# Two more classes may fall within a pair, one class is gone, and some code is aligned and ordered anew: a nested self-attention kernel on one core

## The chip, the cores and the metric

The kernel runs on one core of a Trainium2 chip. The metric is the time of one execution on the device in microseconds (us); before the change the median of three runs is 331.35 us (331.15 to 332.71). PE is the matrix engine (TensorE), DVE is VectorE, ACT is ScalarE, POOL is GpSimd; SP (SyncE) here issues most of the loads, the transposes and part of the stores.

## The reference

The reference is self-attention over 32 sequences of different lengths, eight heads of 64:

```python
for b in range(batch):
    seq_len = lengths[b]
    x_b = x[b, :seq_len].copy()
    qkv = np.matmul(x_b, w_qkv)
    q, k, v = np.split(qkv, 3, axis=-1)
    # each to (n_heads, seq_len, head_dim)
    scores = scale * np.matmul(q, k.transpose(0, 2, 1))
    scores_max = np.max(scores, axis=-1, keepdims=True)
    attn = np.exp(scores - scores_max)
    attn = attn / (np.sum(attn, axis=-1, keepdims=True) + 1e-08)
    out_b = np.matmul(attn, v).transpose(1, 0, 2).reshape(seq_len, dim)
    output[b, :seq_len] = out_b
```

The output is zero from `seq_len` on. x is 32 x 512 x 512 in float32. The lengths are drawn at random from 64 to 511, with a fixed seed; sorted from long to short they are 502 447, 446 436, 363 357, 351 347, 343 333, 323 315, 310 261, 260 257, 246 230, 223 220, 216 183, 164 152, 143 140, 134 119, 101 86, 79 75.

## The kernel before

**Sorting and classes.** The prologue sorts the sequences on the device, longest first, and takes them in 16 pairs, as they stand above. A pair has a class, the smallest number of rows in `CLASSES` (96 to 512 in steps of 32, and 340) that holds its first sequence. Both sequences of a pair are worked at that number of rows. Where the second one fits the next lower class, the pair may "fall": its second half is worked at the lower class. `drops` lists the classes that may fall; before, these are classes of at most 384 rows whose next lower class has as many tiles of 128 rows. A code per pair, twice the class's place in the list plus one where the pair falls, is worked out on the device: POOL makes the column `inner` (1 for thresholds to which a pair may fall, -99 for others), PE multiplies it with the comparisons `le`, and DVE makes `codes` from it.

**Bodies.** For every class there is code for one pair, written by `make_body(N, M, W)`: N rows in the first half, M in the second, W for the batch that is projected in the second half. A half, `half(pr, h, T, N, W, st)`, attends one sequence (scores on PE into `psc`, exponentials on ACT into `ep`, products with `v_aug` on PE into `pav` or `pa`, division on DVE into `onat`) and, in the same stretch of code, projects the next sequence (Q, K and V from `xT` and `w_r`, moved out of PSUM by DVE and ACT). The order of these pieces is written out by hand as a string of tokens for each number of tiles T (`ORDER`, `DENSE`, `FOUR`, `FOUR_SIDES`): at T = 4 with 512 or 480 rows it is `ORDER[4]`, with 448 or fewer one of the `FOUR` strings, in which projections run in two row halves side by side ("cross" products). Where the last tile holds at most 64 rows (`half_rows`), its V projection is made in two column halves side by side (`vsides`). With one tile (T = 1) a half is 32 projections, eight attention products, one V projection and the scores of the next sequence.

**What follows what.** `graph` lays the classes out one behind another, for PE, ACT and DVE each; register compares on the pair's code lead from one body to the next. For PE, targets of jumps are marked ahead (`hint`, `expect`) and code is aligned (`align`); for ACT and DVE one alignment stands at the lead of the first class (`LEAD`). Two-tile pairs keep their scores in another layout than one-tile pairs, so between them PE runs `bridge`: it makes the scores of the next sequence anew in the one-tile layout. `settled` stands beside it.

**Feeding.** SP works by the class alone and doesn't see falls: for each sequence it loads x (`load`), waits until POOL has cast it to f16 (`s_xc`) and until PE is done with the old `xT` (`s_xtf`), and issues a transposing DMA for each tile (`to_xT`), all in its own order, with stores between them. A sequence is loaded five ahead and transposed about two ahead. At one tile, SP transposes into a spare part of `xT` (`stage`) and POOL copies it into place.

**Prologue.** While weights and the first two sequences arrive, DVE casts and copies; behind the last V of the first sequence it makes the two mask tables (`mask_table`, for all 32 sequences) and reads its first code (`begin_loops`).

Of the kernel before, what the change touches and what calls it, by code (L numbers as in the profile page):

```python
# [13 lines left out]
P = 128  # L14
NH = 8
HD = 64
NPAIR = 4
# [14 lines left out]
CLASSES = sorted([STEP * k for k in range(3, 17)] + [DENSE_ROWS], reverse=True)  # L32
FETCH = 256
LEAD = {"act": 0, "dve": 52}


class Prog:
# [52 lines left out]
    def run_part(self, e, a, b, then=None, late=None):  # L90

        b = len(self.ops["pe"]) if b is None else b
        wide = self.wide(a, b)
        for k in range(a, b):
            self.ops["pe"][k](e)
            if then is not None and k == wide[0]:
                then()
            if late is not None and k == wide[-1]:
                late()
# [62 lines left out]
def kernel(  # L162
# [518 lines left out]
    def attn_one(pr, h, ends):  # L681
# [21 lines left out]
        for j in range(2):  # L703
            pr.take("dve", s_od[h][j], 16)

# [17 lines left out]
        for done, w in enumerate(parts):  # L723
            mult(w, done)

# [34 lines left out]

    def half(pr, h, T, N, W, st, last=False):

        g = 1 - h
        tiles = -(-W // P)
        pr.signals += [s_vf[g]] if T == 1 else [s_xtf[h], s_vf[g]]
# [16 lines left out]
        if T == 1:  # L782
            start_proj()
            qk(pr, "a0", g, [(i, 0) for i in range(NPAIR)], W, P)
            qk(pr, "a1", g, [(i, 1) for i in range(NPAIR)], W, P, "act")
            attn_one(pr, h, False)
            vwhole(pr, g)
            read_class(pr, h)
            for b in ("a0", "a1"):
                acquire(pr, b)  # L790
            pr.signals.append(s_xtf[g])
            pr.take("pe", s_on[g])
            scores(pr, h, g, 0, 0, 1, W)
            act_store(pr, h, 0, T)
            return
# [21 lines left out]
        for tok in toks:  # L817
# [40 lines left out]
            elif k == "O":  # L858
                if T == 2 and h == 1:
                    pr.take("act", s_of[0][1])  # L860
                    pr.add("act", lambda e: store(
                        e, e.snap(regs_act["first"], min_val=0, max_val=B - 1), 0, 1, T))
# [3 lines left out]
            else:  # L866
# [36 lines left out]
                for b in bs:  # L903
                    give(b)
                    st["holds"][b] = (g, i) if k in "FGHIQKqk" else (g, "V")
# [37 lines left out]
    def make_body(N, M, W, last=False, turn=None):  # L943
# [50 lines left out]
    def make_prologue():  # L994
# [98 lines left out]
        copy(1, "dve")  # L1093
        cast_x(2)
# [64 lines left out]
        for tok in "Q2 K2 S0 S1 Q3 K3 V0 S2 S3 V1 X2 V2 X3 V3".split():  # L1159
# [25 lines left out]
        pr.add("dve", mask_table)  # L1185
        pr.take("pe", s_on[0])
        return pr

# [23 lines left out]
    def mask_table(e):  # L1212
        q = Chain(e, s_self)
        mask(q, masks[:, 0:B, 0, :], n_k[:, 1 : B + 1])
        mask(q, masks[:, 0:B, 1, :], n_s[:, 0:B])
        q.signal(s_tab)
# [5 lines left out]
    def turn(N):  # L1222
        order = list(stay[lower[N]].middle)
        if is_dense(N) != is_dense(lower[N]):
# [4 lines left out]
    drops = {N: make_body(N, lower[N], lower[N], turn=turn(N)) for N in CLASSES  # L1229
             if lower[N] < N and -(-lower[N] // P) == -(-N // P) and N <= 3 * P}  # L1230
    drops_to = [lower[N] for N in drops]
# [47 lines left out]
    def graph(e, name, opening=None, before=None):  # L1279
# [13 lines left out]
        def align(N, slots, off=0):  # L1293
# [5 lines left out]
            elif 3 * P < N <= FOUR_ROWS:  # L1299
                slot = AT_FOUR  # L1300
# [5 lines left out]
        drop = [N in drops for N in CLASSES]  # L1306
        assert tiles[n - 3 :] == [2, 1, 1]
# [7 lines left out]
        marks = {}  # L1315
# [20 lines left out]
        def goes(k, part, c):  # L1336

            if c == 2 * k + 2:
                return part == "drop"
            if c == 2 * k + 3:  # L1340
                return k + 1 < n and drop[k + 1]
            return k + 2 < n and (k + 2 != one or before is None)
# [52 lines left out]
        def lay_drop(k):  # L1395

            N, body = CLASSES[k], drops[CLASSES[k]]
            codes = (2 * k + 3, 2 * k + 4, 2 * k + 2)
# [3 lines left out]
            if tiles[k] == 1:  # L1402
                if fetch:
                    body.run_part(e, 0, body.second[name], lambda: entry(k))
                else:
                    body.run_half(name, e, 0)
                leave_ = label(k, "gone") if fetch else label(n, "bye")
                e.br_cmp(cur, 2 * n, label(k, "dropped"), leave_, "IS_NE")
                if fetch:
                    bye(k, "gone")  # L1410
                open_(label(k, "dropped"))
                body.run_half(name, e, 1)
                e.br(label(k + 1, "first"))
                return
            if fetch:
                body.run_part(e, 0, body.second[name], lambda: entry(k),
                              lambda: expect("drop", k, codes))
            else:
                body.run_half(name, e, 0)
            body.run_half(name, e, 1)  # L1420
            if goes(k, "drop", codes[0]):
                go("drop", k, codes[0], label(k + 1, "drop"), label(k, "drop_b"))
                open_(label(k, "drop_b"))
            go_first("drop", k, k + 1, label(k, "drop_c"))
            open_(label(k, "drop_c"))
            if goes(k, "drop", codes[1]):
                go_first("drop", k, k + 2, label(k, "drop_d"))
                open_(label(k, "drop_d"))
            align(N, SECOND, -1)
            e.br(label(k + 1, "tail"))  # L1430

        def tail(k):
# [4 lines left out]
            if before is not None and k + 2 == one:  # L1437
                e.br_cmp(cur, 2 * one, label(k + 1, "tail"), label(k + 1, "lead"), "IS_GE")
# [20 lines left out]
        for k, N in enumerate(CLASSES):  # L1459
            T, codes = tiles[k], (2 * k + 3, 2 * k + 4)  # L1460
            final_class = k == n - 1
            if not final_class:
# [3 lines left out]
                if not fetch and k == 0:  # L1466
# [680 lines left out]
```

## Time and profile before

| | |
|---|---|
| runs | 332.71, 331.35, 331.15 us; median 331.35 |
| profiled execution, span on the core | 330.1 us, 1.25 below the median of the runs |
| PE busy | 316.4 us (96%) |
| ACT busy | 242.4 us (73%) |
| DVE busy | 203.6 us (62%) |
| POOL busy | 68.7 us (21%) |
| DMA | 72.42 MB, mean 219 GB/s |
| first pair (0), on PE | 24.56 to 62.84 us |
| pair 13 on PE, its two halves | 300.13 to 310.67 us; the bridge up to 311.96 |

The span runs from the first to the last instruction of the profiled execution. A row of the timeline gives the start in us, the busy time, the engine, the source line, the operation, output<-input, and the count; in brackets the idle time ahead of it and what ended it. DVEq, ACTq, SPq and so on are the engines' sequencers, which wait for semaphores and issue DMAs.

### The profile page before, as it was taken

Reading aid. Unit: us, or ns where it says so; the run is one execution under the profiler, and the core shown is the slowest. Engines: PE = TensorE matmul, PEld = TensorE weight load, DVE = VectorE, ACT = ScalarE, POOL = GpSimd, SP = SyncE. Lnnn points to the kernel's source line nnn. Section 1 sums busy time; section 2 is a strip of 40 time slices with the busy share of each in tenths; the row PEclk is TensorE's granted clock in tenths of the full one; section 3 lists DMA queues with packets and bytes.
Section 4 is the critical chain, followed back from the end, with each engine's and each line's share of the span. In section 5 each row is a group of like instructions: output and inputs, shape, how many; then the busy total and the mean of one; then the engine's idle time right before and its main releaser. Section 6 shows DMA issues by size and latency. Waiting matters only on the chain. (4 is left out here: it accounts for less than half of the span.)

```text
span 330.1 us, 12320 instructions
## 1 busy us (share of the span) xinstructions
PE 316.4 (96%) x4353; PEld 205.5 (62%) x4354; DVE 203.6 (62%) x587; ACT 242.4 (73%) x358; POOL 68.7 (21%) x135
## 2 busy tenths in 40 slices
PE   7899999999999999999999999999999999999880
PEld 2565445455565656656666677677777777677750
DVE  3576576656585575576476557655755566767662
ACT  4577878788889879878778887787677676566531
POOL 3452220201111201210220222022111131131331
PEclk9999999999999999999999999999999999999996
DMA  6957599987656996985997999897689979965952
GB/s 195 341 138 263 94 375 310 292 179 279 153 194 142 326 263 145 323 286 149 283 314 169 235 319 216 214 291 235 212 139 174 214 199 183 170 201 148 200 145 70
DMA packets 83289, 72.42 MB, mean 219 GB/s; under 512 B 41660, under 2 KB 64188, under 8 KB 83204
## 3 DMA queue, kind: packets, MB, share of 16 engines
q1 hardware_dynamic: 69700, 58.27, 70.0%
q10 hardware_dynamic: 13504, 13.11, 11.8%
q8 instruction: 42, 0.69, 0.8%
q14 instruction: 43, 0.35, 0.4%
HBM read 25.32 MB, written 36.70 MB: 188 GB/s over the span
## 5 line engine op out<-in xcount | busy, mean ns | idle before, releaser
L367 ACT ACTIVATE ep<-psc 128x896 f16<-128x896 f32 (+9 forms) x184 | 146.8, 847 | 44.0 <-PE psc L324 34.0
L324 PE MATMUL pa<-xT,w_r 128*128 128x160 f16 (+19 forms) x952 | 127.8, 277 | 1.2 <-PEq L62 1.2
L324 PEld LDWEIGHTS pa<-xT,w_r 128*128 128x128 f16 (+1 forms) x952 | 73.0, 97 | 29.2 <-issue 10.1
L324 PE MATMUL psc<-qkT 64*128 64x224 f16 (+17 forms) x700 | 66.7, 285 | 0.6 <-ACT ep L408 0.4
L324 PE MATMUL pa<-w_r,xT 128*128 128x512 f16 (+4 forms) x332 | 58.6, 328 | 0.3 <-DVE v_aug L560 0.3
L324 PE MATMUL pav<-xT,w_r 64*128 64x352 f16 (+12 forms) x384 | 58.3, 306 | 0.0
L440 DVE CAST qkT<-pa 128x512 f16<-128x512 f32 (+9 forms) x59 | 33.4, 566 | 40.0 <-PE pa L324 36.2
L408 ACT ACTIVATE ep<-psc 128x864 f16<-128x864 f32 (+3 forms) x56 | 49.7, 946 | 10.9 <-PE psc L324 6.5
L324 PE MATMUL pav<-v_aug,ep 128*128 128x65 f16 x1268 | 54.9, 194 | 1.7 <-PEq L62 1.7
L1968 POOL MEMSET v_aug<- 128x256 f16 x28 | 8.8, 313 | 225.5 <-POOLq L1519 225.5
L324 PEld LDWEIGHTS pav<-v_aug,ep 128*128 128x128 f16 x1268 | 48.8, 98 | 10.0 <-issue 3.0
L439 ACT CAST qkT<-pa 128x320 f16<-128x320 f32 (+8 forms) x74 | 34.2, 466 | 16.6 <-PE pa L324 10.8
L661 DVE SCALAR_TENSOR_TENSOR onat<-pav,masks,rcp 128x128 f32<-128x128 f32 (+1 forms) x120 | 41.4, 384 | 4.1 <-DVE rcp L638 1.6
L1962 POOL CAST x<-x_nat 128x1536 f16<-128x1536 f32 (+3 forms) x33 | 42.0, 1272 | 8.6 <-POOLq L1519 8.3
L324 PEld LDWEIGHTS psc<-qkT 64*128 64x128 f16 x700 | 26.7, 94 | 27.2 <-issue 16.7
L463 DVE TENSOR_TENSOR v_aug<-pa,masks 128x512 f16<-128x512 f32 (+1 forms) x46 | 30.8, 674 | 15.0 <-PE pa L324 14.4
L324 PEld LDWEIGHTS pav<-xT,w_r 64*128 64x128 f16 (+1 forms) x384 | 29.8, 95 | 11.6 <-issue 1.6
L324 PEld LDWEIGHTS pa<-w_r,xT 128*128 128x128 f16 (+2 forms) x332 | 22.9, 99 | 18.3 <-issue 4.9
L324 PE MATMUL pav<-w_r,xT 128*128 128x512 f16 (+3 forms) x132 | 24.0, 333 | 0.0
L638 DVE RECIPROCAL rcp<-pav 128x8 f32<-128x8 f32 (+2 forms) x66 | 12.9, 195 | 17.5 <-PE pav L324 14.7
L324 PEld LDWEIGHTS pa<-v_aug,ep 128*128 128x128 f16 x524 | 19.3, 98 | 6.3 <-issue 2.6
L440 DVE CAST qkT<-pav 128x352 f16<-128x352 f32 (+7 forms) x27 | 14.4, 539 | 14.1 <-PE pav L324 13.4
(99 smaller groups left out, 181.4 us busy)
## 6 DMA issues: line engine op xcount, KB each, us to landing
out_dram<-zt SPq DMA_DIRECT2D x16, 768.0 KB, 5.7
x_nat<-in_x_dram SPq DMA_DIRECT2D x12, 512.0 KB
out_dram<-onat ACTq DMA_DIRECT2D x21, 256.0 KB, 3.8
x_nat<-in_x_dram SPq DMA_DIRECT2D x5, 1024.0 KB
out_dram<-onat ACTq DMA_DIRECT2D x12, 384.0 KB, 4.8
out_dram<-onat SPq DMA_DIRECT2D x12, 384.0 KB, 4.4
x_nat<-in_x_dram SPq DMA_DIRECT2D x17, 256.0 KB, 6.5
x_nat<-in_x_dram SPq DMA_DIRECT2D x4, 768.0 KB
```

The lines of the kernel that those rows point to most:

```text
L324: return lambda e: e.matmul(o, lhsT, rhs, start=start, stop=stop)
L367: return e.activation(out=dst[at], in_=src[at], func=AF.Exp, scale=scale)
L408: lambda e, par=par, b=b: e.activation(out=ep[:, i, par, 0:T, 0:N], in_=psc_f[:, par, 0 : T * N].rearrange("p (t n) -> p t n", n=N), func= ...
L439: return lambda e: e.copy(out=dst, in_=src)
L440: return lambda e: e.tensor_copy(out=dst, in_=src)
L463: return lambda e: e.tensor_tensor(out=v_aug[h][:, t, lo // HD : lo // HD + n, 0:HD], in0=area[b][:, 0:w].rearrange("p (a d) -> p a d", d=HD),
L638: pr.add("dve", lambda e: e.reciprocal(out=rv, in_=den).then_inc(s_r, 1))
L661: ins = e.scalar_tensor_tensor(scalar=now[0][:, 1, t : t + 1], op0=ALU.mult, op1=ALU.mult, **ops)
L1962: e.tensor_copy(out=x16[h][:, 0:T, :], in_=x_nat[h][:, 0:T, :]).then_inc(s_xc[h], 1)
L1968: e.memset(v_aug[h][:, T - 1, NPAIR:NH, 0:HD], 0.0)
```

## The change

- The class of 480 rows is gone; the one below 512 is 448.
- A pair of class 512 may fall to 448, and one of 160 to 128, from two tiles to one. For these `drops_at` names where each class falls to.
- A pair that falls from two tiles to one gets new code: behind its first half `fall` makes the scores of the second sequence in the one-tile layout, and `half_one` (what `half` did at T = 1, now a function) runs the second half. DVE clears the second tile of `onat` there, since SP and ACT still store two tiles. After such a pair there is no `bridge`.
- PE marks the jump into the fall of 512 ahead, in the prologue (`hint_drop`). In the falls with four tiles the marks of the next jumps are set in the second half, after some 100 matmuls.
- ACT's and DVE's code is aligned at the lead of the second class (448) instead of the first, at other offsets.
- DVE makes the mask tables behind the copy of tile 1, without the semaphore waits of `Chain` between them, and reads its first code behind K2.

The core of the diff:

```diff
-CLASSES = sorted([STEP * k for k in range(3, 17)] + [DENSE_ROWS], reverse=True)
+CLASSES = sorted([STEP * k for k in range(3, 17) if k != 15] + [DENSE_ROWS], reverse=True)
-LEAD = {"act": 0, "dve": 52}
+LEAD = {"act1": 62, "dve1": 90}
...
+        if falls:
+            pr.add("dve", lambda e: e.memset(onat[h][:, :, 1, :], 0.0))
...
+        if falls:
+            pr.add("dve", lambda e: e.memset(small, 0.0).then_inc(s_of[h][1], 1))
...
+    def half_one(pr, h, W, falls=False):
+
+        g = 1 - h
+        pr.signals.append(s_vf[g])
+        pr.take("pe", s_xt[g], 64)
+        pr.signals.append(s_x16f[g])
+        qk(pr, "a0", g, [(i, 0) for i in range(NPAIR)], W, P)
+        qk(pr, "a1", g, [(i, 1) for i in range(NPAIR)], W, P, "act")
+        attn_one(pr, h, False, falls)
+        vwhole(pr, g)
+        read_class(pr, h)
+        for b in ("a0", "a1"):
+            acquire(pr, b)
+        pr.signals.append(s_xtf[g])
+        pr.take("pe", s_on[g])
+        scores(pr, h, g, 0, 0, 1, W)
+        if falls:
+            store_first(pr)
+        act_store(pr, h, 0, 2 if falls else 1)
+
+    def fall(pr, st, M):
+
+        for b, (_, what) in st["holds"].items():
+            if what != "V":
+                acquire(pr, b)
+        acquire(pr, "s0")
+        pr.signals.append(s_xtf[1])
+        scores(pr, 0, 1, 0, 0, 1, M)
...
-            half(pr, h, T, (N, M)[h], (M, W)[h], st, last and h == 1)
+            if h and T == 2 and M <= P:
+                half_one(pr, h, W, True)
+            else:
+                half(pr, h, T, (N, M)[h], (M, W)[h], st, last and h == 1)
+            if not h and T == 2 and M <= P:
+                fall(pr, st, M)
...
         pr.add("dve", first_masks)
         copy(1, "dve")
+        pr.add("dve", mask_table)
...
+            if tok == "K2":
+                pr.add("dve", lambda e: begin_loops(e))
             if tok == "Q2":
                 pr.add("pe", lambda e: begin_loops(e))
+                pr.add("pe", hint_drop)
...
-        pr.add("dve", mask_table)
...
+    drops_at = {N: M for N, M in lower.items()
+                if M < N <= 3 * P and (-(-M // P) == -(-N // P) or M == P)}
+    drops_at.update({N: FOUR_ROWS for N in CLASSES if N > FOUR_ROWS})
...
-    drops = {N: make_body(N, lower[N], lower[N], turn=turn(N)) for N in CLASSES
-             if lower[N] < N and -(-lower[N] // P) == -(-N // P) and N <= 3 * P}
+    drops = {N: make_body(N, M, M, turn=turn(N, M)) for N, M in drops_at.items()}
...
-            elif 3 * P < N <= FOUR_ROWS:
+            elif N > 3 * P:
                 slot = AT_FOUR
...
-                if not fetch and k == 0:
-                    e.addr_align(FETCH // 2, offset=LEAD[name], max_nops=0)
+                if f"{name}{k}" in LEAD:
+                    e.addr_align(FETCH // 2, offset=LEAD[f"{name}{k}"], max_nops=0)
```

**First place, PE, the second half of pair 0.** The names: `psc` scores, `pa` and `pav` the banks that hold projections and attention products, `xT_0` the next sequence. Before, the second half that leads out of class 512:

```order
L324 MATMUL psc<-qkT_1 128x512 x4
L324 MATMUL pa<-xT_0,w_r 128x480
L324 MATMUL pav<-v_aug_1,ep 128x65 x8
L324 MATMUL pa<-xT_0,w_r 128x480
L324 MATMUL pav<-v_aug_1,ep 128x65 x8
L324 MATMUL pa<-xT_0,w_r 128x480
L324 MATMUL pav<-v_aug_1,ep 128x65 x8
```

After, the end of the first half and the begin of the second in the body that falls from 512 to 448:

```order
L327 MATMUL psc<-qkT_1 128x448 x4
L327 MATMUL pa<-w_r,xT_1 64x256 x8
L327 MATMUL pa<-xT_1,w_r 128x448 x4
L327 MATMUL psc<-qkT_1 128x448 x2
L327 MATMUL pav<-xT_0,w_r 128x448
L327 MATMUL pa<-xT_0,w_r 128x448
L327 MATMUL pav<-xT_0,w_r 128x448
L327 MATMUL pa<-xT_0,w_r 128x448
```

The last V tile of the first half is now `64x256 x8` (`vsides`), and the second half starts with cross products of 448 columns in both banks, where attention products stood between projections.

**Second place, PE, the second sequence of pair 13 and what follows.** Before, the second half that leads out of class 160 (the bridge's eight scores stand behind it, after jumps):

```order
L324 MATMUL psc<-qkT_1 128x160 x8
L324 MATMUL pa<-xT_0,w_r 128x128 x16
L324 MATMUL pav<-v_aug_1,ep 128x65 x16
L324 MATMUL pa<-xT_0,w_r 128x128 x8
L1241 ISA
L1245 TENSOR_LOAD codes
L324 MATMUL psc<-qkT_1 128x160 x4
L324 MATMUL psc<-qkT_0 128x128 x4
L324 MATMUL pa<-w_r,xT_0 128x256 x4
L324 MATMUL pa<-xT_0,w_r 128x128 x8
L324 MATMUL pav<-v_aug_1,ep 128x65 x16
L324 MATMUL pa<-w_r,xT_0 128x256 x4
```

After, the second half of the body that falls from 160 to 128:

```order
L327 MATMUL psc<-qkT_1 128x128 x8
L327 MATMUL pa<-xT_0,w_r 128x128 x32
L327 MATMUL pav<-v_aug_1,ep 128x65 x8
L327 MATMUL psc<-w_r,xT_0 128x512 x4
L1286 ISA
L1290 TENSOR_LOAD codes
L327 MATMUL psc<-qkT_0 128x128 x8
L1393 COMPARE_AND_BRANCH x3
```

The first row is `fall`. Attention takes 8 products instead of 32, and there are 16 scores instead of 16 and the bridge's 8; the eight that `bridge` made stand in the last row of matmuls.

**Third place, DVE, the prologue.** Before, the work behind the first sequence's V:

```order
L532 TENSOR_TENSOR v_aug<-pa,masks 128x4x2x64
L151 TENSOR_TENSOR masks<-row_f,n_k 128x32x4
L151 TENSOR_TENSOR masks<-row_f,n_s 128x32x4
L1257 TENSOR_LOAD codes
L1457 UNCONDITIONAL_BRANCH
```

After, from the first copy on:

```order
L1066 COPY xT<-psc 128x4x128
L1234 TENSOR_TENSOR masks<-row_f,n_k 128x32x4
L1234 TENSOR_TENSOR masks<-row_f,n_s 128x32x4
L1105 CAST x_0<-x_nat 128x512
L1105 CAST x_0<-x_nat 128x256
L1066 COPY xT<-psc 128x2x128
L1093 CAST qkT<-pa 128x512 x2
L1093 CAST qkT<-pav 128x512 x2
L443 CAST qkT<-pa 128x512 x2
L1302 TENSOR_LOAD codes
L443 CAST qkT<-pa 128x512
```

The tables stand ahead of the casts of tiles 2 and 3, and the read of the codes between the evacuations of K2 and Q3.

More of the change, by code (lines that the diff above doesn't have):

```diff
@@ L679, in attnv, with attn_one @@
         return todo
-    def attn_one(pr, h, ends):
+    def attn_one(pr, h, ends, falls=False):
         for v in (f"s{h}",) + halves_av:
@@ L782, in half @@
         if T == 1:
[L783 to L794, printed above, removed]
+            half_one(pr, h, W)
             return
@@ L1212, in mask_table @@
     def mask_table(e):
[L1213 to L1216, printed above, removed]
+        mask(e, masks[:, 0:B, 0, :], n_k[:, 1 : B + 1])
+        mask(e, masks[:, 0:B, 1, :], n_s[:, 0:B])
+        e.nop().then_inc(s_tab, 1)
     stay = {N: make_body(N, N, N) for N in CLASSES}
@@ L1314, in graph @@
         mids = {k: [] for k in range(n)}
-        marks = {}
+        marks = {("tail", -1, 1): [regs["opened"]]} if fetch else {}
         def hint_mid(k):
@@ L2109, in _ @@
             prologue.run("dve", e)
-            begin_loops(e)
             graph(e, "dve")
```

99 lines of the change are left out of this document (64 added, 35 removed).

## The prediction

> **What bounds the kernel now.** I read the page first, then PE's waits, then the stretches of the pairs that the change touches, then the rows around them.
>
> ```profile
> span 330.1 us, 12320 instructions
> PE 316.4 (96%) x4353; PEld 205.5 (62%) x4354; DVE 203.6 (62%) x587; ACT 242.4 (73%) x358; POOL 68.7 (21%) x135
> PE pav L324 <- PEq L62: 1.7, 2, 1.0
> PE pa L324 <- PEq L62: 1.2, 2, 0.9
> PE psc L324 <- ACT ep L408: 0.4, 1, 0.4
> ```
>
> PE is busy 96% of the span. Its waits inside the loops are three lines: 0.4 us behind ACT, and 1.7 and 1.2 us in its own sequencer at L62, the wait that `take` puts in. So up to the last pairs, time taken from PE is time taken from the end, unless what feeds PE then comes late. The span is 330.1 us and the median of the runs 331.35: the sum is made on the span, and the 1.25 us around it are kept.
>
> Columns of the next view: stretch, its length, busy time of PE (instructions), PEld, DVE, ACT, POOL, clock, DMA.
>
> ```profile
> 24.56:43.95 19.39, 19.39 (x210) 9.47 (x210) 12.42 (x28) 15.50 (x16) 4.31 (x4) 1.00 0.71 197
> 43.95:62.84 18.89, 18.89 (x209) 9.61 (x208) 12.48 (x34) 15.24 (x16) 2.29 (x3) 1.00 1.14 314
> 62.84:80.43 17.59, 17.57 (x245) 10.05 (x245) 10.89 (x33) 14.33 (x20) 2.29 (x3) 1.00 0.88 263
> 300.13:305.95 5.82, 5.82 (x93) 4.37 (x92) 4.20 (x13) 3.66 (x7) 1.44 (x3) 1.00 0.66 205
> 305.95:310.67 4.72, 4.72 (x89) 3.97 (x88) 3.04 (x9) 3.47 (x7) 1.43 (x3) 1.00 1.15 158
> 310.67:311.96 1.29, 0.41 (x10) 0.26 (x10) 1.15 (x3) 0.16 (x1) 0.00 (x0) 1.00 0.81 196
> 311.96:314.81 2.85, 2.85 (x53) 2.11 (x53) 1.49 (x4) 1.41 (x3) 1.38 (x3) 1.00 0.54 166
> ```
>
> In order: pair 0 (two halves at 512 rows; the next batch is projected at 512 columns, then 480), the first half of pair 1 (all at 448), pair 13 (two halves at 160, projecting 160, then 128 columns), the bridge, and the first half of pair 14. PE fills every stretch but the bridge, at a clock of 1.00.
>
> **Pair 0.** The lengths are 502 and 447, so the pair may now fall to 448. Its first half still attends 502 rows, but projects batch 1 at 448 columns. 512 to 480 columns took the half from 19.39 to 18.89, so 64 columns are worth 1.00. The last V tile also shrinks, as `half_rows(448)` holds:
>
> ```profile
> 42.11 1.04 PE L324 MATMUL pa<-w_r,xT 128*128 128x512 f16 x4
> 42.99 1.03 PE L324 MATMUL pa<-xT,w_r 128*128 128x512 f16 x4
> 73.98 0.63 PE L324 MATMUL pav<-w_r,xT 128*64 128x256 f16 x8
> 74.54 0.67 PE L324 MATMUL pa<-v_aug,ep 128*128 128x65 f16 x16
> ```
>
> From start to next start the whole tile takes 0.88, its two sides 0.56: 0.32 less. The second half becomes what pair 1's first half is: 17.59 for 18.89, 1.30 less. **Together 1.00 + 0.32 + 1.30 = 2.62 us**, all on PE. ACT (15.5 of 19.4) and DVE do less as well.
>
> What is late next is batch 3's rows. SP issues their four transposes in one go:
>
> ```profile
> 48.50 8.37 SPq L1603 DMA_TRANSPOSE xT<-x  x4
> xT<-x SPq DMA_TRANSPOSE x80, 3.8
> ```
>
> The last is issued some 1.3 before 56.87; with the median of 3.8 to landing that is 59.4. PE needs them 0.4 into pair 1, at 63.2 before and 60.6 after. 1.2 us of cover are left; without it each microsecond of delay costs one. I take nothing, and 0 to 1.3 as its bounds (the second half's gain).
>
> **Pair 13.** The lengths are 134 and 119. Its first half gets the shape of the second of before (W = 128): 4.72 for 5.82, **1.10 less**. Behind it `fall` makes batch 27's scores once more for one tile, and `half_one` runs it as a single tile:
>
> ```profile
> 306.34 1.20 PE L324 MATMUL pa<-xT,w_r 128*128 128x128 f16 x16
> 307.37 0.65 PE L324 MATMUL pav<-v_aug,ep 128*128 128x65 f16 x16
> 311.96 1.52 PE L324 MATMUL pa<-xT,w_r 128*128 128x96 f16 x32 [0.88 <-PEq L62]
> 313.31 0.42 PE L324 MATMUL pav<-v_aug,ep 128*128 128x65 f16 x8
> 313.57 1.03 PE L324 MATMUL psc<-w_r,xT 128*128 128x512 f16 x4
> 314.53 0.34 PE L324 MATMUL psc<-qkT 64*128 64x96 f16 x8
> ```
>
> By distances between starts: `fall` 0.41 (as the bridge's PE time), 32 projections of 128 columns 2 x 1.03 = 2.06, attention 0.26, V 0.96, scores about 0.36: 4.05. Before, the second half, the bridge's work and its wait took 4.72 + 1.29 = 6.01. So PE could begin pair 14 at 311.96 - 1.10 - 1.96 = 308.9, **3.06 us earlier**. DVE gets one clearing of `onat` (512 elements):
>
> ```profile
> 1.17 0.48 DVE L2071 MEMSET zt<- 128x512 f32 x1 [1.05 <-PEq L2128]
> ```
>
> 0.48 in a half where DVE is busy about half the time (1.49 of 2.85): nothing.
>
> But the wait of 0.88 ahead of pair 14 was for batch 29's rows, and SP isn't made faster:
>
> ```profile
> 302.71 1.21 SPq L1603 DMA_TRANSPOSE xT<-x  x1
> 306.84 1.22 SPq L1603 DMA_TRANSPOSE xT<-x  x1
> 315.06 0.42 SPq L1527 DMA_DIRECT2D out_dram<-onat  x1
> SPq L1519 <- SPq L1519: 4.5, 4, 2.4
> ```
>
> The last row is SP's waiting from 280 to the end, 4.5 us in four: SP mostly runs on without pause, and its transposes of 306.84 follow from its own queue. Against pair 0's shift, which moves SP's last waits too, it keeps its place. The rows were there shortly before 311.96, 5.1 after the issue. The median of 3.8 gives 310.6; then pair 14 begins 1.3 earlier, not 3.06. The ends: 0 (5.1 again) and 3.06 (2.1 after the issue; batch 28's, issued at 302.71, were used at 306.34, so 3.6 or less is seen). I take the median, as most rows of that kind lie there.
>
> By the Trainium skill, "DMA: Bandwidth & Descriptors", section "Anatomy of one DMA — SWDGE (gpsimd) path", a DMA costs about 2.0 us fixed plus its bytes over 436 GB/s; an estimate from it for 128 KB is 2.3 us, which would land these rows at 309.1 and bring 2.8 instead of 1.3. The trace's 3.8 is far above that, so the sum doesn't use it.
>
> Behind pair 14's begin the tail is a chain too:
>
> ```profile
> 310.19 1.48 ACTq L1527 DMA_DIRECT2D out_dram<-onat  x2
> 312.67 0.61 POOL L1962 CAST x<-x_nat 128x512 f16<-128x512 f32 x1
> 317.90 0.21 DVE L708 RECIPROCAL rcp<-pav 128x8 f32<-128x8 f32 x1 [1.53 <-DVEq L62]
> ```
>
> DVE's 1.53 at 317.90 is for batch 27's second store, which SP issues only at 315.06, behind the staging of batch 31 and so behind POOL's cast at 312.67, which pair 14's begin releases. They move with pair 14, so **1.3 us** reaches the end.
>
> **The rest, cost at nothing.** The two mask tables move on DVE from behind the last V to behind the second copy:
>
> ```profile
> 11.55 0.43 DVE L1069 CAST x<-x_nat 128x512 f16<-128x512 f32 x1 [0.94 <-DMA x_nat<-in_x_dram]
> 25.31 0.28 DVE L151 TENSOR_TENSOR masks<-row_f,n_k 128x128 f32<-128x128 f32 x1
> 27.39 0.69 DVE L440 CAST qkT<-pa 128x512 f16<-128x512 f32 x1 [1.35 <-PE pa L324]
> 18.89 0.69 DVE L440 CAST qkT<-pa 128x512 f16<-128x512 f32 x1 [0.82 <-PE pa L324]
> ```
>
> Two of 0.28, less than 0.6 us, go into the 0.94 in which DVE waited for a load. Where they stood, DVE afterwards waited 1.35 for PE: nothing is won there. Its read of the codes moves into the 0.82 before 18.89. Either would cost its overrun if the gap closed: up to 0.6. POOL gets one more select on `inner`:
>
> ```profile
> 3.94 0.19 POOL L151 TENSOR_SCALAR_AFFINE_SELECT inner<-inner 128x1 f16<-128x1 f16 x1 [0.22 <-POOLq L143]
> 6.93 0.17 PE L2057 MATMUL pa<-le,ones_c 14*1 14x32 f16 x1
> ```
>
> 0.41 with its wait; PE takes `inner` at 6.93, over 2 us later. Code alignment of ACT and DVE moves jumps on engines that idle 27 and 38%:
>
> ```profile
> ACT ep L367 <- issue: 0.8, 2, 0.4
> ```
>
> 0.8 us of ACT's idle time before exponentials has no releaser; between -0.8 and +0.8 in all, behind PE: nothing.
>
> **Sum:** 2.62 + 1.3 = 3.9; 330.1 becomes 326.2 and the median **327.4 us**.
>
> **Rivals.**
> - *One saving is lost.* Batch 29's rows again take 5.1, or batch 3's and the tail each give back about half: 331.35 - 2.62 = 328.7. For it: DMA shares of 1.14 and 1.15 in the stretches with those transposes. Against: the median.
> - *Both are kept whole.* Batch 29's rows land by 308.9: 331.35 - 2.62 - 3.06 = 325.7. For it: batch 28's 3.6 or less; against: 3.8, and the store by SP behind it.
> - *Slower: cold jumps on PE.* PE now jumps into the fall of 512, from there into 448, and from the fall of 160 into that of 128, to code not in line. The kernel marks each target ahead. If the marks don't work, each jump waits for code from memory, like the smallest transfer:
>
> ```profile
> len_c<-in_lengths_dram ACTq DMA_DIRECT2D x1, 0.2 KB, 1.9
> ```
>
> Three at 1.9 are 5.7 against 3.9 won: 333.2. It decides above 1.3 a jump. Against it: PE's waits show 2.9 us at L62 in all, though it jumps at every pair. The Trainium skill, "Runtime: NRT & Kernel Launch", section "Instruction fetch mechanics", says that a taken branch beyond the two pages held waits for the target's page; the trace's marked jumps show at most those 2.9 us of it, and no run here shows an unmarked one.
> - *Nothing falls.* If the flags come out zero, only the 480 class is gone: 448 columns for 480 in one half, 0.5: 330.9. Against it: 447 is at most 448, 119 at most 128, and falls of that kind run already at 96 to 340.
>
> **How the numbers follow.** Forecast 0.60; one saving lost 0.17; both whole 0.12; cold jumps 0.06; nothing falls 0.05. The range goes from below 325.7 to above 328.7 with some 0.5 for landing times on either side: 325.2 to 329.3. It leaves out the last two. A measurement can tell 0.5% (1.66 us) from no change: faster is below 329.7, which holds the first three but for their ends, 0.88; same 0.06; slower 0.06.
>
> **What will show it.** Pair 0: projections at 448 from the first half on, no 480, and its two halves near 18.1 and 17.6 with no PE wait at the first cross product of pair 1. Pair 13: eight scores of 64x128, 32 projections of 128x128, and then how long PE stands at L62 ahead of the 96-column projections: about 1.7 by my forecast, none if it is whole, 3 if it is lost. The masks stand near 10.6 to 11.2 on DVE. It is wrong if PE waits at the new jumps, or if the first scores of pair 0 start later than 24.56.

## The result, and the profile after

The changed kernel takes 331.39 us in the median of 22 runs (326.52 to 337.86, and one run of 1433.65), the kernel before 332.15 us beside it (329.11 to 335.02, 22 runs): 0.9977 by these medians. The forecast was 327.4 us, in a range of 325.2 to 329.3. The ratio of the table below is 0.9931, with a 95% interval of 0.9905 to 0.9957: 0.7% faster, where 0.988 was forecast. Ten of the changed kernel's runs and the outlier lie over 1.5% above its fastest and are left out of the ratio; their mean granted clock is low (0.972 to 0.987, against 0.986 to 0.994), which the experiments below tie to the fall of 160, so medians of all runs are given beside the ratios. The profiled execution is one of the long ones: 334.17 us, span 332.5.

The head of the page and PE's waits, of the changed kernel (us in total, times, longest):

```profile
span 332.5 us, 12315 instructions
PE 312.5 (94%) x4353; PEld 204.9 (62%) x4354; DVE 201.1 (60%) x586; ACT 240.2 (72%) x357; POOL 69.1 (21%) x136
PE pa L327 <- PEq L62: 6.1, 4, 2.8
PE psc L327 <- issue: 0.7, 2, 0.5
PE pav L327 <- DVE v_aug L563: 0.3, 1, 0.3
```

PE's busy time fell by 3.9 us (316.4 to 312.5); the span didn't. The forecast's 3.9 is the span's: from PE's work its steps take 2.62, 1.10 and 5.13 - 4.05 = 1.08, together 4.80, so it is chance that the two numbers agree. PE's wait at L62 ahead of projections grew from 1.2 to 6.1 us. By stages, first before, then after (stretch, its length, busy time of PE and the others, clock, DMA):

```profile
62.84:300.13 237.29, 236.29 (x3417) 159.24 (x3417) 149.07 (x449) 185.22 (x280) 42.12 (x72) 1.00 0.86 222
305.95:311.96 6.01, 5.13 (x98) 4.23 (x98) 4.19 (x12) 3.63 (x8) 1.43 (x3) 1.00 1.08 166
311.96:330.10 18.14, 9.37 (x164) 6.78 (x164) 7.81 (x17) 4.97 (x11) 5.42 (x12) 0.84 0.41 120
```

```profile
24.45:42.58 18.13, 18.13 (x216) 9.72 (x214) 11.34 (x26) 14.86 (x16) 4.31 (x4) 1.00 0.73 188
42.58:61.16 18.58, 17.73 (x245) 9.97 (x245) 11.91 (x37) 14.79 (x20) 2.44 (x3) 1.00 1.12 315
61.16:298.54 237.38, 236.10 (x3418) 158.61 (x3418) 149.42 (x450) 186.02 (x280) 42.09 (x72) 1.00 0.87 224
298.54:307.39 8.85, 6.15 (x90) 5.20 (x90) 3.18 (x11) 3.61 (x7) 1.55 (x3) 0.81 0.64 180
307.39:313.94 6.55, 3.74 (x62) 2.83 (x61) 3.79 (x9) 2.76 (x5) 1.43 (x3) 1.00 0.71 128
313.94:332.50 18.56, 9.49 (x164) 6.84 (x164) 7.76 (x16) 4.05 (x9) 5.34 (x12) 0.83 0.36 108
```

Pair 0's halves are 18.13 and 18.58; the twelve pairs behind it take what they took; pair 13 takes 8.85 + 6.55 = 15.40 where it took 5.82 + 6.01 = 11.83, and in its first half the clock is 0.81. PE's timeline at the begin of pair 13 before, then from the same scores on after, where it shows both stalls:

```profile
300.13 0.45 PE L324 MATMUL psc<-qkT 64*128 64x160 f16 x8
300.51 1.41 PE L324 MATMUL pa<-xT,w_r 128*128 128x160 f16 x16
```

```profile
298.54 0.45 PE L327 MATMUL psc<-qkT 64*128 64x160 f16 x8
301.68 1.30 PE L327 MATMUL pa<-xT,w_r 128*128 128x128 f16 x16 [2.70 <-PEq L62]
302.77 1.09 PE L327 MATMUL pav<-v_aug,ep 128*128 128x65 f16 x16
303.67 1.04 PE L327 MATMUL pa<-xT,w_r 128*128 128x128 f16 x8
305.92 0.61 PE L327 MATMUL pa<-xT,w_r 128*128 128x128 f16 x8
306.37 0.65 PE L327 MATMUL pav<-v_aug,ep 128*128 128x65 f16 x16
310.73 0.40 PE L327 MATMUL psc<-qkT 64*128 64x128 f16 x8
313.94 1.52 PE L327 MATMUL pa<-xT,w_r 128*128 128x96 f16 x32 [2.81 <-PEq L62]
```

The **first stall**, 2.70 us, is for batch 27's rows. PE's scores ahead of it came 1.59 earlier than before (298.54 for 300.13), the rows 1.39 later (301.55 for 300.16), though SP had issued their second transpose 1.02 earlier (296.81 for 297.83). Behind the stall the same products take 1.09 where they take 0.65 some 3.6 us later, and eight projections 1.04 for 0.61: the trace's record of the clock has 0.5 from 302.35 to 305.76. The **second stall**, 2.81 us, is put down to L62 as well, but the rows of batch 29 had landed at 310.41. The records of PE's sequencer and of its code fetches tell why it came so late to that wait:

```
306.81         mark for the jump into the fall of 128 (L1358)
310.72  3.06   the branch that jumps there (L1393)
311.44  0.96   code fetch, 16 KB
313.83         PE's sequencer takes batch 29's rows (L62)
```

Here 2.81 us are lost to a **cold jump**: the branch waited for the code that it leads to. (Below, a jump is called cold where its branch took over 2 us, warm where it took under 1.) That branch took 3.06 us; PE's other branches inside the loops took 0.06 to 0.70, the two other new jumps (at 23.93 and 60.09) 0.47 and 0.46.

### The profile page after: what moved, and what is told of

It reads as the page before. It is cut to its first block, busy times and chain, and to the rows that moved or that the text cites. A ratio compares the mean times of both kernels' runs of the same rounds, so it can differ in the third digit from the quotient of the medians.

```text
span 332.5 us, 12315 instructions
## 1 busy us (share of the span) xinstructions
PE 312.5 (94%) x4353; PEld 204.9 (62%) x4354; DVE 201.1 (60%) x586; ACT 240.2 (72%) x357; POOL 69.1 (21%) x136
## 5 line engine op out<-in xcount | busy, mean ns | idle before, releaser
L370 ACT ACTIVATE ep<-psc 128x896 f16<-128x896 f32 (+8 forms) x182 | 143.7, 837 | 41.4 <-PE psc L327 31.1
L327 PE MATMUL pa<-xT,w_r 128*128 128x160 f16 (+19 forms) x952 | 124.0, 276 | 6.3 <-PEq L62 6.1
L327 PEld LDWEIGHTS pa<-xT,w_r 128*128 128x128 f16 (+1 forms) x952 | 72.7, 97 | 31.9 <-issue 14.2
L327 PE MATMUL psc<-qkT 64*128 64x448 f16 (+16 forms) x692 | 66.8, 285 | 1.4 <-issue 0.7
L327 PE MATMUL pav<-xT,w_r 64*128 64x352 f16 (+12 forms) x416 | 65.5, 309 | 0.3 <-DVE v_aug L563 0.3
L327 PE MATMUL pa<-w_r,xT 128*128 128x512 f16 (+4 forms) x316 | 55.0, 326 | 0.1
L443 DVE CAST qkT<-pa 128x448 f16<-128x448 f32 (+8 forms) x52 | 28.5, 548 | 39.1 <-PE pa L327 35.2
L327 PE MATMUL pav<-v_aug,ep 128*128 128x65 f16 x1180 | 51.1, 194 | 1.0 <-PEq L62 1.0
L327 PEld LDWEIGHTS pav<-v_aug,ep 128*128 128x128 f16 x1180 | 45.4, 98 | 8.0 <-issue 2.2
L327 PEld LDWEIGHTS psc<-qkT 64*128 64x128 f16 x692 | 27.0, 94 | 27.8 <-issue 16.5
L327 PEld LDWEIGHTS pav<-xT,w_r 64*128 64x128 f16 (+1 forms) x416 | 32.4, 94 | 13.1 <-issue 1.8
L664 DVE SCALAR_TENSOR_TENSOR onat<-pav,masks,rcp 128x128 f32<-128x128 f32 (+1 forms) x108 | 37.7, 384 | 3.8 <-DVE rcp L641 1.5
L327 PEld LDWEIGHTS pa<-w_r,xT 128*128 128x128 f16 (+2 forms) x316 | 21.7, 99 | 16.3 <-issue 5.6
L443 DVE CAST qkT<-pav 128x352 f16<-128x352 f32 (+7 forms) x31 | 16.9, 551 | 19.1 <-PE pav L327 18.3
L327 PEld LDWEIGHTS pa<-v_aug,ep 128*128 128x128 f16 x588 | 21.8, 98 | 7.2 <-issue 3.0
L327 PE MATMUL pav<-w_r,xT 128*128 128x512 f16 (+3 forms) x144 | 26.1, 331 | 0.0
L327 PE MATMUL pa<-v_aug,ep 128*128 128x65 f16 x588 | 25.1, 194 | 0.1
```

What stands on the lines that cost most here:

```text
L327: return lambda e: e.matmul(o, lhsT, rhs, start=start, stop=stop)
L370: return e.activation(out=dst[at], in_=src[at], func=AF.Exp, scale=scale)
L443: return lambda e: e.tensor_copy(out=dst, in_=src)
L664: ins = e.scalar_tensor_tensor(scalar=now[0][:, 1, t : t + 1], op0=ALU.mult, op1=ALU.mult, **ops)
```

## The experiments

Times are medians of all runs; the kernel before gave 332.51 to 333.08 in these comparisons.

| kernel | us (runs) | ratio and 95% interval | mean clock |
|---|---|---|---|
| the change | 331.39 (22) | 0.9931 (0.9905 to 0.9957) | 0.986 |
| after_again | 330.22 (12) | 0.994 (0.9911 to 0.997) | 0.988 |
| mark_early | 330.86 (12) | 0.9933 (0.9901 to 0.9965) | 0.986 |
| mark_late | 331.86 (12) | 0.9967 (0.9931 to 1.0002) | 0.984 |
| only_160 | 333.07 (12) | 1.001 (0.9965 to 1.0056) | 0.988 |
| border | 330.8 (12) | 0.9963 (0.9929 to 0.9997) | 0.988 |
| border_sp | 328.11 (6) | 0.9892 (0.9844 to 0.994) | 0.993 |
| border_mark | 328.8 (12) | 0.9886 (0.9854 to 0.9918) | 0.991 |
| border_mark_again | 330.9 (12) | 0.9931 (0.9893 to 0.9968) | 0.989 |
| border_mark_sp | 329.71 (8) | 0.9914 (0.9874 to 0.9954) | 0.988 |
| both_lead | 332.31 (12) | 0.9967 (0.9929 to 1.0005) | 0.987 |
| only_512 | 330.44 (12) | 0.9952 (0.9924 to 0.998) | 0.993 |
| only_512_lead | 329.37 (11) | 0.991 (0.9881 to 0.9939) | 0.994 |
| only_512_lead_again | 329.93 (12) | 0.991 (0.9874 to 0.9946) | 0.992 |
| only_512_old | 333.35 (14) | 0.9999 (0.9967 to 1.0031) | 0.991 |

**One fall at a time.** `only_512` leaves out the fall of 160, `only_160` the fall of 512:

```diff
-                if M < N <= 3 * P and (-(-M // P) == -(-N // P) or M == P)}
+                if M < N <= 3 * P and -(-M // P) == -(-N // P)}
```

```diff
-    drops_at.update({N: FOUR_ROWS for N in CLASSES if N > FOUR_ROWS})
...
-                pr.add("pe", hint_drop)
...
```

> Edit: the fall of 160 to 128 is taken away, all else is as changed. Theory 'pair 0's saving is real and kept up to the tail': ratio to the kernel before 0.992 (2.6 us less), PE stands under 1 us for batch 27's rows. Theory 'feed' (what PE gains in pair 0, it gives back where SP's transposes of the last pairs come late): PE stands 1 to 2.7 us ahead of pair 13, and the ratio is 0.997 to 1.0. No branch of over 0.8 us ahead of the end in either.

> Edit: the fall of 512 to 448 and its mark are taken away, all else is as changed (448 columns for 480 in the second half of pair 0, 0.5 us). Theory 'cold jump': the branch into the fall of 128 takes about 3 us, eats the 3.06 that the fall takes from PE, and the ratio is 0.997 to 1.0. Theory 'feed': PE stands under 1 us ahead of pair 13, no halved clock there, and the runs scatter as little as the kernel before (2 us), where the changed kernel's scatter by 6 and more.

With the fall of 512 alone no stall stands ahead of pair 13, the clock is 1.00 up to the tail, and all runs lie within 3.5 us (329.09 to 332.59): its gain reaches the end, though it is smaller (0.9952) than expected (0.992). With the fall of 160 alone the branch takes 3.21 us and PE's clock is halved behind it (timeline of `only_160`):

```profile
307.39 0.40 PE L327 MATMUL psc<-qkT 64*128 64x128 f16 x8
310.81 2.30 PE L327 MATMUL pa<-xT,w_r 128*128 128x96 f16 x32 [3.02 <-PEq L62]
312.91 0.64 PE L327 MATMUL pav<-v_aug,ep 128*128 128x65 f16 x8
```

The 32 projections take 2.30 instead of 1.52. The ratio is 1.001: alone, this fall gains nothing. That the cold jump eats its saving isn't shown: the last of batch 29's rows landed at 310.29, 0.36 ahead of the branch's end (310.65), so with a warm jump PE would have stood 2.50 here too, unless the rows had then come earlier. The mean clock is low here too (0.988) and high in `only_512` (0.993), so the windows of half clock come with this fall and not with pair 0's earlier arrival, against 'feed'.

**Where the mark stands.** `mark_early` sets the mark at the fall's first projection, `mark_late` in its second half:

```diff
-                    body.run_part(e, 0, body.second[name], lambda: entry(k), ahead)
+                    body.run_part(
+                        e, 0, body.second[name],
+                        lambda: (entry(k), ahead() if ahead else None), None)
```

```diff
-                    body.run_part(e, 0, body.second[name], lambda: entry(k), ahead)
+                    body.run_part(e, 0, body.second[name], lambda: entry(k), None)
...
+                if fetch and ahead:
+                    body.run_part(e, body.second[name], None, ahead)
...
```

> Edit: the mark for the jump from the fall of 160 into the fall of 128 is set at the first projection of the fall's first half, some 9 us ahead of the jump instead of 3.9. The jump's branch took 3.06 us in the changed kernel, and PE stood 2.81 us. Theory 'too late' (a marked target needs about 6 to 7 us to arrive: 3.9 + 3.06 = 7.0): the branch falls to 0.3 to 0.7, the stall to 0.3 to 0.6, and the median from 331.4 to about 329. Theory 'mark lost' (PE's own code, read on past a border between mark and jump, pushes the target out): branch stays at 2.5 to 3.1, median 331.4. Theory 'rows' (PE waits for batch 29's rows, as the prediction has it): the branch may fall, but PE then stands about 1.7 at L62.

> Edit: the same mark is set in the fall's second half, behind its first 16 projections, some 2.4 us ahead of the jump. Theory 'too late': the branch takes 3 to 4.6 us, the median is 331.4 to 333. Theory 'mark lost': if the border lies ahead of the new place, the branch falls to 0.3 to 0.7 and the median to about 329; if behind it, 2.5 to 3.1 as in the changed kernel. Theory 'rows': PE stands about 1.7 at L62 whatever the branch does.

With the mark 9.4 us ahead the branch still took 2.10, with 2.9 us ahead 3.73. 'Too late' falls with the first (it had 0.3 to 0.7); besides, in the changed kernel the jump at 297.63 had its last mark at 292.21, 5.4 ahead, and took 0.42. 'Mark lost' had 2.5 to 3.1 for the first, more than the 2.10. 'Rows' isn't ruled out in `mark_early`: batch 29's rows landed at 308.94, the branch was over at 309.29. In `mark_late` they had landed (311.08) before the branch began (311.38).

**Borders of the code.** PE's code is fetched in blocks of 16 KB (one packet of q8 below), which the kernel's alignment counts as 256 instructions (`FETCH`). From its aligned start the fall of 160 runs over a border some 60 instructions ahead of the jump. `border` moves the start (and so the border) with the early mark, `border_mark` with the mark as changed, which then stands behind the border; `border_sp` is `border` with one transpose less on SP.

```diff
             if tiles[j] == 1:
+                if fetch and tiles[k] > 1:
+                    e.addr_align(FETCH, offset=100, max_nops=0)
```

```diff
-                        to_xT(1, N, 2)
+                        if N == 160:
+                            to_xT(1, P, 1)
+                        else:
+                            to_xT(1, N, 2)
```

> Edit: the mark for the jump out of the fall of 160 as in mark_early (first projection), and the fall's code begins at place 100 of a block of 256 instructions, so that it runs over a border some 160 instructions ahead of the jump instead of some 60, and over none behind it. Theory 'border' (a marked target is fetched only when PE's code runs over the next border, and can be used about 5 us later): a 16 KB fetch of code shows near 303, the branch takes 0.3 to 0.7 instead of 2.1 to 3.7. Theory 'mark does not hold' (jumps of this form are always cold): the branch takes 2 to 3.7, with the fetch behind its start. On the time, theory 'SP's rows' (pair 13's last rows and pair 14's come no earlier): PE stands at L62 instead, 1 to 3 in all ahead of and behind pair 13's second half, and the ratio is that of only_512, 0.993 to 0.996, with the clock near 0.99. Theory 'jump alone cost the gain': the ratio is 0.988 to 0.991.

> Edit: the fall of 160 begins at place 100 as in border, but its mark stays at the last projection of its first half, so that it stands behind the border, and no border follows up to the jump. Theory 'border': no fetch between mark and jump, the branch takes 2.5 to 3.7, the ratio is 0.995 to 1.0. Theory 'a mark fetches by itself, but slowly' (about 7 us): the fetch shows ahead of the branch, which takes 2 to 3. If the branch takes 0.7 or less, both are wrong.

> Edit: border, and SP transposes only the first tile of batch 27 (its 119 rows lie in it, and nothing reads the second tile where the pair falls); SP's other work is as changed. Takes 1.2 us of issue from SP ahead of batch 28's rows. Theory 'SP's rows': batches 28 and 29 land 1.0 to 1.5 earlier against PE's start of pair 13, PE stands that much less at L62, and the time is 1.0 to 1.5 below border's. Rival 'the transposes' way to landing' (DMA, not SP's issue, sets when rows come): less than 0.5 below border.

My theory of borders was wrong both ways: `border` should have been warm and took 2.62, `border_mark` should have been cold and took 0.44. The DMA view of `border_mark` from the mark (302.35) on, up to 304.5, and that of the changed kernel from its mark (306.8) up to 311.3, past the branch's start:

```profile
q1 hardware_dynamic: 697, 0.34, 56.8%
q10 hardware_dynamic: 89, 0.09, 11.6%
q8 instruction: 2, 0.03, 7.8%
```

```profile
q1 hardware_dynamic: 704, 0.17, 18.8%
q10 hardware_dynamic: 272, 0.26, 16.5%
q14 instruction: 1, 0.01, 0.4%
```

q8 is PE's code, 16 KB a packet (q14 is another engine's). Behind a mark with no border between it and the jump, code is fetched soon, here 0.5 and 1.3 us later; in the changed kernel none is until the branch has begun. `border_sp`, with the same PE code as `border`, was warm (0.37): there a fetch came at 302.87, 4.0 ahead of the branch. By medians it is 2.69 us faster than `border`, where 'SP's rows' had 1.0 to 1.5; as its jump was warm too, SP's part isn't told apart. In `border` the cold jump itself cost next to nothing: batch 29's rows landed at 308.37, the branch was over at 308.32.

**The same again, and SP relieved.** Unedited, the changed kernel and `border_mark`; and `border_mark` with the SP edit above.

> No edit: the changed kernel once more, on the chip of the runs beside it. Theory 'place' (where the code stands against borders and the mark decides whether the jump out of the fall of 160 is cold): the branch takes 2 to 3.7 again, ratio 0.990 to 0.996, clock near 0.9865. Theory 'chance of the run' (whether the marked code comes in time is a matter of one execution): the branch may take 0.3 to 0.7 in this profile.

> No edit to border_mark (the fall of 160 begins at place 100, its mark stays at the last projection of its first half, no border between mark and jump). Theory 'a mark is read at once where no border follows it': code is fetched within 1.5 of the mark, the branch takes 0.3 to 0.7 again, ratio 0.986 to 0.992, most runs below 329. Theory 'chance of the run': the branch takes 2 or more, and the ratio goes to 0.993.

> Edit: border_mark, and SP transposes only the first tile of batch 27, as in border_sp. Theory 'SP's rows': with the jump cheap and SP 1.2 ahead, PE waits under 1 for the rows of batches 28 and 29 together, and the ratio is 0.984 to 0.987, 1.0 to 1.5 us below border_mark. Rival 'code fetches' (the last of 16 landings is late by 1.5 where a code fetch falls together with it, whatever SP does): within 0.5 us of border_mark.

The branch took 3.41 in `after_again`; 0.49 in `border_mark_again` and 0.44 in `border_mark_sp`. Between `border` and `border_mark` only the place of the mark differs. In all traces with this jump, it was warm in 4 of 4 with the mark behind the last border (0.44 to 0.49: the four with `border_mark`'s PE code), and cold in 6 of 7 with the mark ahead of it (2.10 to 3.73: the change twice, only_160, mark_early, mark_late, border); the seventh is `border_sp` with 0.37. So the place of the mark goes with it but doesn't settle it alone. But the time of `border_mark_again` went back to 0.9931: PE stood 4.09 for batch 27's rows, and `after_again` had stood 2.85 there. The SP edit's gain, 0.9914 against 0.9931 in one comparison, lies within the intervals: inconclusive. 'SP's rows' had 0.984 to 0.987, and under 1 us of waiting for batches 28 and 29; PE stood 1.22 for batch 29's rows alone.

**DVE's earlier read.** Both kernels here lack the fall of 160. `only_512_old` has masks, DVE's `begin_loops` and both alignments as before; `only_512_lead` only the alignments:

```diff
-LEAD = {"act1": 62, "dve1": 90}
+LEAD = {"act0": 0, "dve0": 52}
```

> Edit: only_512, with the mask tables, DVE's read of the codes and the alignment of ACT's and DVE's code as in the kernel before. The prediction costs these edits at nothing: the ratio is that of only_512 (0.9952) within 0.002, and pair 0's first scores start between 23.7 and 24.7 in both. Rival 'these edits carry part of the gain or of a loss': the ratio moves by over 0.003, or the start of pair 0 by over 0.6 beyond that spread.

> Edit: only_512 with the alignment of ACT's and DVE's code as in the kernel before; the mask tables and DVE's read of the codes stay where the change puts them. In only_512_old DVE's jump into the fall of 512 began at 27.3 and its next work at 30.1 (PE stood 2.25), in only_512 the jump was at 24.2 and the next work at 26.1. Theory 'read earlier' (the earlier read lets the cold jump run while DVE waits for PE anyway): jump near 24.2, no stall of PE over 0.6 in the first 10 us of pair 0, ratio 0.993 to 0.997. Theory 'alignment': PE stands 1 to 2.3 there, ratio 0.998 to 1.001.

The edits that I had at nothing are worth 2.9 us by the medians (330.44 to 333.35), 1.6 by the ratios, whose intervals overlap. Against `only_512_lead` (0.9881 to 0.9939) that of `only_512_old` (0.9967 to 1.0031) lies clear. DVE's timeline in `only_512_old`, then in `only_512_lead_again`, around its jump into the fall of 512:

```profile
25.55 0.28 DVE L154 TENSOR_TENSOR masks<-row_f,n_k 128x128 f32<-128x128 f32 x1
25.99 0.29 DVE L154 TENSOR_TENSOR masks<-row_f,n_s 128x128 f32<-128x128 f32 x1 [0.15 <-DVEq L146]
30.14 0.62 DVE L443 CAST qkT<-pa 128x448 f16<-128x448 f32 x1 [3.86 <-issue]
```

```profile
24.42 0.69 DVE L535 TENSOR_TENSOR v_aug<-pa,masks 128x512 f16<-128x512 f32 x1
26.45 0.62 DVE L443 CAST qkT<-pa 128x448 f16<-128x448 f32 x1 [1.33 <-PE pa L327]
```

DVE has no marks. In `only_512_old` it jumps at 27.3 and works again at 30.14; PE stands 2.25 for that cast ("PE pa L327 <- DVE qkT L443"), and its clock is halved from 31.21 to 34.62. With the masks ahead and the codes read at K2 the jump starts some 3 us earlier and is over when PE delivers. Masks and read weren't tried apart. The alignment isn't what matters: 0.991 without it.

**The fall of 160 with a cheap jump, or not at all.** `both_lead` is `border_mark` with that alignment, `only_512_lead_again` is unedited.

> Edit: border_mark (both falls, the mark of the jump out of the fall of 160 behind the last border) with the alignment of ACT's and DVE's code as in the kernel before. Theory 'rows and clock' (with the jump cheap, what the fall of 160 takes from PE is still given back to late rows of batches 27 to 29 and to windows of half clock): branch 0.3 to 0.7, mean clock 0.989 to 0.991, ratio within 0.003 of only_512_lead_again or above it. Rival 'the jump was all': ratio 0.003 to 0.005 below only_512_lead_again (1.0 to 1.6 us).

> No edit to only_512_lead, beside both_lead on the same chip. Theory 'pair 0 alone': ratio 0.990 to 0.996, mean clock 0.992 to 0.994, no stall of over 1.2 ahead of the tail, runs within 4 us of each other. If the ratio lies above 0.998, pair 0's saving isn't kept either.

Stages of `both_lead` (pair 0; pairs 1 to 12; pair 13 in two parts; from pair 14 on), then of `only_512_lead_again`:

```profile
23.73:60.07 36.34, 35.84 (x459) 19.69 (x458) 23.16 (x62) 29.51 (x35) 6.79 (x7) 1.00 0.92 253
60.07:297.63 237.56, 235.68 (x3417) 159.04 (x3417) 149.35 (x450) 186.04 (x280) 42.20 (x72) 1.00 0.86 224
297.63:307.84 10.21, 6.17 (x89) 5.44 (x89) 3.29 (x11) 3.50 (x7) 1.55 (x3) 0.83 0.60 161
307.84:312.42 4.58, 3.80 (x61) 2.87 (x62) 3.67 (x9) 2.33 (x5) 1.43 (x3) 1.00 0.50 101
312.42:332.10 19.68, 9.38 (x164) 6.80 (x164) 7.77 (x17) 4.48 (x10) 5.39 (x12) 0.84 0.41 121
```

```profile
24.22:60.55 36.33, 35.92 (x459) 19.68 (x458) 23.22 (x62) 29.72 (x35) 6.79 (x7) 1.00 0.92 250
60.55:297.24 236.69, 235.90 (x3417) 159.08 (x3417) 149.31 (x450) 185.91 (x280) 42.13 (x72) 1.00 0.89 226
297.24:303.06 5.82, 5.82 (x93) 4.37 (x93) 4.20 (x13) 3.66 (x7) 1.47 (x3) 1.00 0.72 208
303.06:308.63 5.57, 5.12 (x97) 4.22 (x97) 3.75 (x11) 3.47 (x7) 1.43 (x3) 1.00 0.95 177
308.63:326.90 18.27, 9.37 (x164) 6.79 (x164) 8.26 (x18) 5.14 (x11) 5.44 (x12) 0.82 0.39 119
```

Pair 0 is alike. With the fall, pair 13's first part takes 10.21 for 5.82: a stall of 4.01 for batch 27's rows, and then half clock. The second part, 4.58 with its cheap jump, is 0.99 shorter than the 5.57 without the fall, a gain far below what the first part lost. By medians `both_lead` is 2.4 us the slower (0.9967 against 0.991, the intervals overlapping from 0.9929 to 0.9946). 'The jump was all' falls.

## Why the prediction was wrong

The steps of the sum on the spans, in us; the forecast's column is worked out from its own steps (18.07 + 17.59 for pair 0; 11.83 - 1.3 for pair 13):

| stage | before | forecast | after | only_512_lead_again |
|---|---|---|---|---|
| up to pair 0 | 24.56 | 24.56 | 24.45 | 24.22 |
| pair 0 | 38.28 | 35.66 | 36.71 | 36.33 |
| pairs 1 to 12 | 237.29 | 237.29 | 237.38 | 236.69 |
| pair 13, up to pair 14 | 11.83 | 10.53 | 15.40 | 11.39 |
| pair 14 to the end | 18.14 | 18.14 | 18.56 | 18.27 |
| span | 330.10 | 326.18 | 332.50 | 326.90 |

- **Pair 0** went the right way, mis-sized. Its first half is 18.13 (18.07 forecast). "The second half becomes what pair 1's first half is", 17.59, was 18.58, with waits of 0.32 for DVE's evacuation of the V sides (L563) and 0.53 ahead of scores; in `only_512_lead_again` pair 0 saves 1.95. So 1.6 to 2.0 came of 2.62. A possible reason, not tried: pair 1's first half follows a half in the same order of pieces, this one follows the order of 512 rows.
- **Pair 13's step failed**: "the median gives 310.6; then pair 14 begins 1.3 earlier". Pair 13 became 3.57 longer: 2.70 of waiting for batch 27, 1.4 more than forecast behind it, nearly all half clock (the first half's 8.85 is 4.72 + 2.70 + 1.43), and 2.81 for the cold jump, less the 0.88 that PE had waited before and some 2.5 that its work shrank. The landing of batch 29, 310.41, came near the forecast (310.6) by luck, as two errors cancelled: SP didn't keep its place, it issued at 307.98 instead of 306.84, and the landing took 2.43 from there, not 3.8. It didn't matter here, as the branch ended 3.4 later. (The prediction's other estimate, 2.3, is worked out for DMAs that GpSimd issues; the median of SP's transposes is 3.8 in this trace too.)
- **Batch 27's rows** were no term at all. Before, PE took them 0.03 after they landed (300.16), with no time to spare. After, PE came 1.59 earlier, and of the 32 increments that tell of these rows 31 were there at 299.90, the last only at 301.55. So 1.65 of the 2.70 is that one late increment; without it PE would have stood about 1.05. I had looked at the rows behind pair 13's first half, not at those at its beginning.
- **The rival of cold jumps** (0.06) came true at one of its three places, at 2.81 of PE's idle time and not 1.9. (PE stood 1.86 to 3.49 there in the other cold traces, but in `only_160`, `mark_early` and `border` batch 29's rows landed only about when the branch ended.) The prediction's own sign of being wrong, a wait of PE at a new jump, is there. I took the 2.9 us at L62 of marked jumps as proof that marks work; they work where they stand right, and here they didn't. The rule in the Trainium skill, "Runtime: NRT & Kernel Launch", section "Instruction fetch mechanics", that a branch outside the two held pages waits for a fetch, agrees: 3.06 us with the 16 KB fetch 0.72 behind the branch's start.
- **Clock.** The forecast kept it at 1.00. `only_512` and `only_512_lead`, without the fall of 160, have a mean clock of 0.992 to 0.994 in three comparisons, the changed kernel 0.986; `only_512_old`, with DVE's stall, has 0.991. As an estimate, 0.007 of 330 us are 2.3 us of PE's time.
- **Masks, read of codes, alignment at nothing**: right for the change as a whole, but for the wrong reason. They are the cover of DVE's cold jump into the fall of 512; without them that fall gains nothing (0.9999).
- POOL's select and DVE's clearing of `onat` cause no wait of PE in the trace, as forecast.

What stays open: why a mark ahead of a border held in `border_sp` and in an older fall (the jump at 297.63) but not in `border`; what a cold jump costs where the rows are late as well; and how much of batch 27's lateness the fall itself causes. A stall of 2.7 to 4.1 there stood in 5 of 10 traces with both falls, and in none of the 5 that lack one of them nor in that of before.

## What to carry to other kernels

Where the work in front of a late transfer is made shorter, ask of every transfer behind it when it lands and when it will be wanted, the one at the very beginning of the shortened stage first. A jump to code that isn't in line has a price of its own, 3 us here, until its branch is seen to be short in the trace; a mark set ahead proves nothing, and an engine without marks needs idle time to jump in. Before a stall is put down to a jump, look when the data behind it landed. Of the versions tried, the fall of 512 alone with the earlier read of DVE's codes (`only_512_lead`) gave 0.991 twice, with intervals that still touch the changed kernel's; `border_mark`'s two, 0.9886 and 0.9931, lie around it.

## What the runs showed of the hardware

- **Half clock after about 2 us of idle PE.** The record of the clock steps in windows of 3.41 us. Up to the tail of all 16 traces, the ten windows in which PE stood 1.98 us or more (2.70 in the changed kernel, all 3.41 in `both_lead`) were each followed by one at 0.5, and none of the others was, though PE stood 1.95 in one of them. The limit isn't that sharp: the windows just ahead of the half clock in which the traces end had 1.87 (`mark_early`) and 1.88 (`only_512_lead_again`) too. Two neighbours of each kind, of `border_mark` and of `after_again`, with PE's busy time behind the length and the clock third from the end:

```profile
303.34:306.75 3.41, 1.43 (x28) 1.35 (x25) 0.77 (x3) 1.08 (x2) 0.89 (x3) 1.00 0.73 237
306.75:310.16 3.41, 3.41 (x30) 2.01 (x29) 2.02 (x5) 0.59 (x1) 0.54 (x1) 0.50 0.39 85
```

```profile
312.01:315.42 3.41, 1.45 (x35) 1.48 (x36) 0.56 (x1) 0.00 (x0) 0.96 (x3) 1.00 0.46 159
315.42:318.83 3.41, 3.41 (x64) 2.48 (x62) 2.24 (x4) 1.49 (x4) 1.81 (x4) 1.00 0.41 115
```

The changed kernel's cold jump passed without it: its 2.81 lay 1.46 in one window and 1.35 in the next. The Trainium skill, "TensorE: Matmul & The Clock Gate", section "HAM oscillation — how this bites in real kernels", warns of idle gaps over about 3.4 us; here 1.98 within one window was enough.
- **Late landings come together with code fetches.** A transpose's landing is told in 16 increments of a semaphore. In the 16 traces together, of 880 transposes between whose issue and landing PE's code was fetched, 112 had the last increment 0.4 us or more behind the one before it, most often 1.5 to 1.6; of 398 without such a fetch, 3. In the changed kernel 31 of batch 27's 32 increments were there at 299.90 and the last at 301.55, with a fetch of PE's code at 299.51. From 225 us on, SP took 1.68 us on average to issue a transpose while PE's code was fetched (212 of them) and 1.25 otherwise (239). This is seen together in the traces; no run moved a fetch alone.
